# Attention in a transformer block: two score blocks at a time, with the order of every engine written out

## The chip, the cores and the metric

The kernel runs on one core of a Trainium2 chip. A core has five engines with a queue each: TensorE (PE; it multiplies matrices, and a transpose is a matmul by a permutation), VectorE (DVE), ScalarE (ACT), GpSimd (POOL) and SyncE (SP, which here only issues DMAs). Matmul results land in PSUM, 8 banks of 128 partitions by 512 floats; everything else works on SBUF. The metric is the device time of one launch, in microseconds (us), as the median of several runs.

## The reference, cut to what matters

A trunk of two layers, each a half-step SwiGLU FFN, a mixer, and another half-step FFN, on 256 tokens of width 1024. The mixer of the first layer is an SSM (Mamba-2); that of the second, which the change concerns, is attention with a window of 128 over a key and value set shared by 8 query heads (16 query heads, 2 key/value groups, head size 64):

```
q = rmsnorm((u @ w_q).reshape(b, t, KV_HEADS, GROUP, HEAD_DIM), q_norm)
...
s = einsum('bqkrd,bskd->bkrqs', qk, kk) * scale + bias
s = where(valid, s, -inf)
m = maximum(max(s), sink)
p = exp(s - m)
denom = sum(p) + exp(sink - m)
o = einsum('bkrqs,bskd->bqkrd', p / denom, vk)
...
return o @ w_o
```

The tokens fall in two tiles of 128 (t = 0, 1). Queries of tile 0 see 128 keys, those of tile 1 see 256.

## The kernel before

All activations are kept transposed, features on partitions. A weight is fetched in units of 1 MB on the SP queue, through three raw buffers, and then split by `Unit.part`: ScalarE rounds it to a high part `wh` (L171), VectorE subtracts to get the low part `wl` (L172). A product of two float32 matrices is three matmuls, high by high, high by low and low by high (`mm3`, `wmm3`). These splits run during the stage for `w_q` (16 parts of 512 columns), for `w_o` (16 parts, as soon as a part of `w_q` has been used for the last time and its buffer is free) and, after it, for the FFN.

The pages' line numbers are those of helpers: L106 is a matmul or transpose issued through `in_turn` while the order is strict, L108 one that isn't; L997 and L993 are VectorE's and ScalarE's instructions that go through `dve` and `act`.

`attention` (L946) works in these steps, for each of four query pieces (row tile t, head group g):

- `q_mm` (L953): one of eight steps k of the query product, three matmuls with 512 columns into a PSUM tile `pq`.
- `q_norm` (L961): ScalarE squares (`qn`, L963), VectorE sums by head (`ss`, L965) and adds epsilon (`me`, L220), GpSimd takes the power -1/2 (`rq`, L222), VectorE scales (`qn`, L968).
- `q_turn` (L973): four transposes into `ptq`, and ScalarE's copy to `qT` (L979).

The heads of a piece are taken in blocks (L982): a block holds 4 heads (t = 0, 128 keys) or 2 heads (t = 1, 256 keys), all of them in one half of the partitions: the two head halves i = b % 2 lie on partitions 0 to 63 and 64 to 127 of `qT` and `kT`. There are 12 blocks. For a block:

- `scores` (L999): one matmul for each head, 64 rows of the array deep, into `ps` (two PSUM buffers); then VectorE copies the sinks into the last column of `sp`, adds the bias and takes the maximum (`tensor_tensor_reduce` into `sp` and `mx`), and negates it (`nmx`).
- `expo` (L1026): ScalarE, one exponential for each head with its sum into `den`.
- `divide` (L1032): VectorE, a reciprocal `rd` and one multiplication for each head.
- `weights_T` (L1040): four transposes into `ptp` (pool `ps_tr`, two banks), ScalarE's copy to `pT`.
- `values` (L1052): matmuls of 64 columns into one half of the partitions of `po` (a bank of `ps_tr` too). After the last block of a (t, g), ScalarE rounds `po` into `uTh` and VectorE subtracts into `uTl`.

A float32 matmul of these steps shows as two matmul records in the trace, with a weight load each.

The order is written by hand at the end of `attention` (L1106 to L1131). While `strict[0]` is set, each TensorE instruction is tied behind the one before it in program order. `act` and `dve` tie ScalarE's and VectorE's instructions of the block steps in two chains in the same way; the norms and copies of the queries and the splits are in no chain, and the scheduler, which lays out each engine's queue when the program is built, puts them where it sees room. `first` gives the block steps a high priority. `F(n)` issues n pieces of filling work: 16 steps of the second head group's queries (with `q_norm` after the 8th and the 16th), then 32 pieces `o_one` of the output projection's first half (L1071), three matmuls each, which read head group 0 of `uTh` and `uTl` for both row tiles. Block n goes through scores at step n, exponentials at n+1, division at n+2, transposes at n+4, values at n+5. `fills` has no filling work for steps 6 to 10. `later(42, cur.stats)` puts the mean of squares, on which the norms rest, behind 42 matmuls.

## Time and profile before

| | us |
|---|---|
| median of 3 runs | 1043.94 (1042.96 to 1044.14) |
| the profiled execution | 1042.34 |
| its span, first to last instruction | 1040.6 |
| TensorE busy | 1028.8 (99%) |
| VectorE busy | 735.1 (71%) |
| ScalarE busy | 602.9 (58%) |
| attention, first query matmul to the second half of the output projection | 767.30 to 838.60 |

A row of the timeline gives the start in us from the first instruction, the length, the engine, the line, the operation, output<-inputs by the program's names, shapes, how many were merged (x), and in brackets the idle time before it with what ended it. PE is a matmul, PEld a weight load. A matmul's shape begins with the rows and columns of the array that it uses (64*128: half of the rows; 128*64: half of the columns). Matmuls overlap, so a matmul's own length is more than the distance to the next one's start. A row of the windows gives each engine's busy us in a stretch and its instructions (x), then TensorE's granted clock, the share of the DMA engines and GB/s. A row of the groups ends with busy us, mean ns of one, and the idle us before them with their releasers. The chain that ended last follows the end back from instruction to instruction, to whatever released each.

### The profile page before, as it was taken

What the parts mean: (1) busy time and instruction counts of PE and PEld (TensorE: products, weight loads), DVE (VectorE), ACT (ScalarE), POOL (GpSimd) and SP (SyncE); (2) the same over time, 40 slices, a digit from 0 to 9 for tenths busy, and PEclk for the clock granted to TensorE, in tenths of its full rate; (3) what the DMA queues carried; (4) which work ended last, traced back from release to release, by engine and by line L of the source; (5) the groups of instructions that cost most, each with busy time, mean ns of one, the idle gap of its engine ahead of it and who ended that gap; (6) DMA issues with size and microseconds to landing.
All of it is one profiled execution on the core that took longest, in us unless ns stands there. A gap on an engine that the chain in (4) does not pass through costs nothing.

```text
span 1040.6 us, 18036 instructions
## 1 busy us (share of the span) xinstructions
PE 1028.8 (99%) x7160; PEld 944.6 (91%) x7160; DVE 735.1 (71%) x1252; ACT 602.9 (58%) x1040; POOL 57.4 (6%) x78
## 2 busy tenths in 40 slices
PE   8899999999999999999999999999999999999998
PEld 8899999999999999999999999999996699888887
DVE  6866656789999988656556975665677678565653
ACT  6564545668976756455545754455567565455551
POOL 1100000003220010000000000100002000000000
PEclk9999999999999999999999999999999999999999
DMA  8676565658564365746465555594641436464641
GB/s 284 172 243 202 165 200 185 180 170 255 166 180 163 124 204 163 234 158 215 163 203 188 177 171 195 174 299 162 217 162 41 123 116 210 162 210 161 221 136 41
DMA packets 139589, 187.19 MB, mean 180 GB/s; under 512 B 5100, under 2 KB 122000, under 8 KB 139504
## 3 DMA queue, kind: packets, MB, share of 16 engines
q1 hardware_dynamic: 137168, 179.32, 52.8%
q0 software_dynamic: 2288, 6.69, 2.4%
q8 instruction: 56, 0.92, 0.4%
q14 instruction: 29, 0.24, 0.1%
q10 hardware_dynamic: 48, 0.02, 0.0%
HBM read 184.90 MB, written 1.11 MB: 179 GB/s over the span
## 4 chain that ended last, share of the span: by engine, by line
PE 91%; DVE 3%; DMA 3%; ACT 1%; SPq 1%; issue 0%; POOL 0%; DVEq 0%; ACTq 0%
PE pm L108 45%; PE acc L108 23%; PE pp L108 9%; PE pa L108 5%; DMA raw<-in_ffn_w_dram 2%; PE pq L106 2%; PE pa L106 1%; PE py L108 1%; DVE wl L172 1%; PE pz L108 1%; PE ps L106 1%; PE po L106 1%; DVE sp L997 1%; SPq L158 1%; PE pkv L108 1%; DMA raw<-in_ssm_w_in_dram 1%
## 5 line engine op out<-in xcount | busy, mean ns | idle before, releaser
L172 DVE TENSOR_TENSOR wl<-raw,wh 128x1024 fp32r<-128x1024 f32 (+1 forms) x372 | 412.2, 1130 | 87.3 <-ACT wh L171 86.9
L171 ACT CAST wh<-raw 128x1024 fp32r<-128x1024 f32 (+1 forms) x372 | 347.5, 970 | 110.5 <-PE acc L108 43.6
L108 PE MATMUL pm<-uT,wh 128*128 128x512 f32 (+1 forms) x1216 | 403.9, 381 | 1.7 <-DVE tp L330 1.6
L108 PE MATMUL pm<-uT,wl 128*128 128x256 f32 x1152 | 321.5, 280 | 0.0
L108 PEld LDWEIGHTS pm<-uT,wh 128*128 128x128 f32 x1216 | 223.6, 188 | 45.3 <-DVE tp L330 2.4
L108 PEld LDWEIGHTS pm<-uT,wl 128*128 128x128 f32 x1152 | 216.6, 188 | 1.0
L108 PE MATMUL acc<-ghl,wh 128*128 128x256 f32 x1056 | 190.6, 281 | 0.6 <-ACT ghl L347 0.6
L339 ACT COPY lo<-pm 128x256 f32<-128x256 f32 x136 | 50.3, 370 | 198.0 <-PE pm L108 198.0
L108 PEld LDWEIGHTS acc<-ghl,wh 128*128 128x128 f32 x1056 | 162.2, 188 | 2.9 <-ACT ghl L347 0.9
L340 DVE TENSOR_TENSOR tp<-pm,lo 128x256 f32<-128x256 f32 x136 | 57.5, 423 | 129.5 <-ACT lo L339 129.4
L108 PE MATMUL acc<-ghl,wl 128*128 128x256 f32 x528 | 148.5, 282 | 0.0
L108 PE MATMUL pp<-uT,wh 128*128 128x256 f32 x576 | 104.8, 283 | 0.1
L108 PEld LDWEIGHTS acc<-ghl,wl 128*128 128x128 f32 x528 | 99.4, 188 | 0.0
L108 PEld LDWEIGHTS pp<-uT,wh 128*128 128x128 f32 x576 | 88.8, 189 | 0.7 <-DVE uT L304 0.3
L108 PE MATMUL pp<-uT,wl 128*128 128x256 f32 x288 | 80.7, 281 | 0.0
L108 PE MATMUL pm<-vh,wh 128*128 128x256 f32 x256 | 73.3, 287 | 1.3 <-ACT wh L171 1.3
L108 PE MATMUL pm<-vh,wl 128*128 128x256 f32 x256 | 72.4, 284 | 0.5 <-DVE wl L172 0.5
L108 PE MATMUL pm<-vl,wh 128*128 128x256 f32 x256 | 72.3, 283 | 0.0
L108 PE MATMUL acc<-wh,ghl 128*128 128x512 f32 x176 | 58.3, 395 | 0.0
L108 PEld LDWEIGHTS pp<-uT,wl 128*128 128x128 f32 x288 | 54.3, 188 | 0.0
L347 ACT CAST ghl<-g 128x256 fp32r<-128x256 f32 x88 | 35.5, 403 | 31.7 <-DVE g L344 31.4
L108 PEld LDWEIGHTS pm<-vh,wh 128*128 128x128 f32 x256 | 48.9, 191 | 1.4 <-ACT wh L171 1.4
(236 smaller groups left out, 1253.5 us busy)
## 6 DMA issues: line engine op xcount, KB each, us to landing
raw<-in_ffn_w_dram SPq DMA_DIRECT2D x168, 512.0 KB, 4.9
raw<-in_ffn_w_dram SPq DMA_DIRECT2D x44, 1024.0 KB, 5.4
raw<-in_ssm_w_in_dram SPq DMA_DIRECT2D x16, 1024.0 KB, 5.5
raw<-in_ssm_w_out_dram SPq DMA_DIRECT2D x8, 1024.0 KB, 5.3
raw<-in_ssm_w_in_dram SPq DMA_DIRECT2D x8, 512.0 KB, 5.1
pr<-pdram POOLq DMA_DIRECT2D x8, 512.0 KB, 4.6
raw<-in_w_q_dram SPq DMA_DIRECT2D x4, 1024.0 KB, 5.0
raw<-in_w_o_dram SPq DMA_DIRECT2D x4, 1024.0 KB, 5.1
```

Source lines behind the costliest of these rows:

```text
L106: r = op(*args, **kw)
L108: r = op(*args, **kw)
L158: nc.sync.dma_start(view(raw, shape, lo, n0)[:, k0:k0 + src.shape[1]], src)
L171: return (nc.scalar.copy(wh, rs).ins, nc.vector.tensor_sub(wl, rs, wh.bitcast(F32)).ins)
L172: nc.vector.tensor_sub(wl, rs, wh.bitcast(F32)).ins)
L339: nc.scalar.copy(lo, pw[:, 256:512])
L340: nc.vector.tensor_add(o, pw[:, 0:256], lo)
L347: nc.scalar.copy(gh, g)
L997: chain[1] = op(*args, **kw).ins
```

## The change

Two blocks, the two head halves of the same heads, are now one pair m (six pairs). In `scores` the matmuls of the two halves alternate, head by head, into two `ps` tiles; in `values` they alternate by key tile, into the two partition halves of `po`. The sink copies move to GpSimd. `sp` and its small companions have six buffers instead of five. `po` of head group 0 lies in `ps_acc` instead of `ps_tr`. The evacuation of `po` is a step of its own (`evacuate`), written behind `expo`.

The query steps are now in the chains: the square and the copy `qT` in ScalarE's, the sums, epsilon and scaling in VectorE's. `q_norm` is cut in two, and `q_scale` is placed by hand. The first head group's query product is done row tile by row tile instead of alternating; the mean of squares comes after 26 matmuls instead of 42.

The order of steps is written out: see the end of the diff. In the loop, pair m goes through scores, then exponentials; pair m-1 is divided behind the scores of m; pair m-2 is transposed, one block on each side of the scores; pair m-3 has its values. The filling steps stand in groups of 5, 3, 4 and 4 (queries), then 10, 8, 8 and the rest (output projection).

```diff
--- before.py
+++ after.py
@@ -958,25 +958,43 @@
         def q_bank():
             return ps_acc.tile([P, 512], F32, tag="acc", name=nm("pq"))
 
+        chain = list(cur.last)
+
+        def act(op, *args, **kw):
+            with behind(chain[0]):
+                chain[0] = op(*args, **kw).ins
+
+        def dve(op, *args, **kw):
+            with behind(chain[1]):
+                chain[1] = op(*args, **kw).ins
+
         def q_norm(pq, t, n):
-            qn = ap.tile([P, 512], F32, tag="qn", name=nm("qn"), bufs=2)
-            nc.scalar.activation(qn, pq, AF.Square, scale=DH ** -0.5)
-            ss = sb.tile([P, 8], F32, tag="ss8", name=nm("ss"), bufs=2)
-            nc.vector.tensor_reduce(out=ss, in_=qn.rearrange("p (g d) -> p g d", g=8),
-                                    axis=AX.X, op=ALU.add)
-            rq = rms_rstd(ss, 8, "rq", cur.eps[:, t:t + 1])
-            nc.vector.tensor_mul(qn.rearrange("p (g d) -> p g d", g=8),
-                                 pq.rearrange("p (g d) -> p g d", g=8),
-                                 rq.unsqueeze(2).to_broadcast([P, 8, DH]))
-            qns[t, n] = qn
+            with tc.high_priority():
+                qn = ap.tile([P, 512], F32, tag="qn", name=nm("qn"), bufs=2)
+                act(nc.scalar.activation, qn, pq, AF.Square, scale=DH ** -0.5)
+                ss = sb.tile([P, 8], F32, tag="ss8", name=nm("ss"), bufs=2)
+                with behind(chain[1]):
+                    chain[1] = nc.vector.tensor_reduce(out=ss, in_=qn.rearrange("p (g d) -> p g d", g=8),
+                                                       axis=AX.X, op=ALU.add).ins
+                me = sb.tile([P, 8], F32, tag="me8", name=nm("me"), bufs=2)
+                dve(nc.vector.tensor_scalar_add, me, ss, cur.eps[:, t:t + 1])
+                rq = sb.tile([P, 8], F32, tag="rstd8", name=nm("rq"), bufs=2)
+                nc.gpsimd.tensor_tensor(out=rq, in0=me, in1=mhalf[:, :8], op=ALU.pow)
+            qns[t, n] = qn, pq, rq
+
+        def q_scale(t, n):
+            qn, pq, rq = qns[t, n]
+            with tc.high_priority():
+                dve(nc.vector.tensor_mul, qn.rearrange("p (g d) -> p g d", g=8),
+                    pq.rearrange("p (g d) -> p g d", g=8), rq.unsqueeze(2).to_broadcast([P, 8, DH]))
 
         def q_turn(t, n):
-            qn = qns[t, n]
+            qn = qns[t, n][0]
             pt = ps_acc.tile([P, 512], F32, tag="acc", name=nm("ptq"))
             for j in range(4):
                 in_turn(nc.tensor.transpose, pt[:, j * P:(j + 1) * P], qn[:, j * P:(j + 1) * P], anti)
             qT = ap.tile([P, 512], F32, tag="qT", name=nm("qT"), bufs=3)
-            nc.scalar.copy(qT, pt)
+            act(nc.scalar.copy, qT, pt)
             qTs[t, n] = qT
 
         blocks = []
@@ -986,56 +1004,48 @@
                 for b in range(8 // nh):
                     blocks.append((t, g, b, nh))
         sps, pTs, pos = {}, {}, {}
-        chain = list(cur.last)
-
-        def act(op, *args, **kw):
-            with behind(chain[0]):
-                chain[0] = op(*args, **kw).ins
-
-        def dve(op, *args, **kw):
-            with behind(chain[1]):
-                chain[1] = op(*args, **kw).ins
-
-        def scores(n):
-            t, g, b, nh = blocks[n]
+        def scores(m):
+            t, g, b, nh = blocks[2 * m]
             qT = qTs[t, g]
             L = (t + 1) * P
-            i = b % 2
             p0 = (b // 2) * nh
-            ps = ps_mm.tile([P, nh, L], F32, tag="mm", name=nm("ps"))
-            sp = ap.tile([P, nh, L + 1], F32, tag="sp", name=nm("sp"), bufs=5)
-            mx = sb.tile([P, 4], F32, tag="mx", name=nm("mx"), bufs=5)
-            nmx = sb.tile([P, 4], F32, tag="nmx", name=nm("nmx"), bufs=5)
-            den = sb.tile([P, 4], F32, tag="den", name=nm("den"), bufs=5)
-            rd = sb.tile([P, 4], F32, tag="rd", name=nm("rd"), bufs=5)
-            hs = [(p0 + x) * 2 + i for x in range(nh)]
+            pss = []
+            for i in range(2):
+                pss.append(ps_mm.tile([P, nh, L], F32, tag="mm", name=nm("ps")))
+                sps[2 * m + i] = [ap.tile([P, nh, L + 1], F32, tag="sp", name=nm("sp"), bufs=6)]
+                for w in ("mx", "nmx", "den"):
+                    sps[2 * m + i].append(sb.tile([P, 4], F32, tag=w, name=nm(w), bufs=6))
             for x in range(nh):
-                j = p0 + x
-                mm(ps[:, x, :], qT[i * DH:(i + 1) * DH, j * P:(j + 1) * P],
-                   kT[g][i * DH:(i + 1) * DH, 0:L], True, True)
-            dve(nc.vector.tensor_copy, sp[:, :, L], snk[:, g * 8 + hs[0]:g * 8 + hs[-1] + 1:2])
-            for x in range(nh):
-                hh = g * 8 + hs[x]
-                dve(nc.vector.tensor_tensor_reduce,
-                    out=sp[:, x, 0:L], in0=ps[:, x, :], in1=bias[g][:, hs[x], S - L:S],
-                    scale=1.0, scalar=snk[:, hh:hh + 1], op0=ALU.add, op1=ALU.max,
-                    accum_out=mx[:, x:x + 1])
-            dve(nc.vector.tensor_scalar_mul, nmx[:, 0:nh], mx[:, 0:nh], -1.0)
-            sps[n] = sp, nmx, rd, den
-
-        def expo(n):
-            sp, nmx, rd, den = sps[n]
-            for x in range(blocks[n][3]):
-                act(nc.scalar.activation, sp[:, x, :], sp[:, x, :], AF.Exp,
-                    bias=nmx[:, x:x + 1], accum_out=den[:, x:x + 1])
-
-        def divide(n):
-            t, g, b, nh = blocks[n]
-            L = (t + 1) * P
-            sp, nmx, rd, den = sps[n]
-            dve(nc.vector.reciprocal, rd[:, 0:nh], den[:, 0:nh])
-            for x in range(nh):
-                dve(nc.vector.tensor_scalar_mul, sp[:, x, 0:L], sp[:, x, 0:L], rd[:, x:x + 1])
+                for i in range(2):
+                    mm(pss[i][:, x, :], qT[i * DH:(i + 1) * DH, (p0 + x) * P:(p0 + x + 1) * P],
+                       kT[g][i * DH:(i + 1) * DH, 0:L], True, True)
+            for i in range(2):
+                sp, mx, nmx, den = sps[2 * m + i]
+                h0 = g * 8 + p0 * 2 + i
+                nc.gpsimd.tensor_copy(sp[:, :, L], snk[:, h0:h0 + 2 * nh - 1:2])
+                for x in range(nh):
+                    dve(nc.vector.tensor_tensor_reduce,
+                        out=sp[:, x, 0:L], in0=pss[i][:, x, :], in1=bias[g][:, (p0 + x) * 2 + i, S - L:S],
+                        scale=1.0, scalar=snk[:, h0 + 2 * x:h0 + 2 * x + 1], op0=ALU.add, op1=ALU.max,
+                        accum_out=mx[:, x:x + 1])
+                dve(nc.vector.tensor_scalar_mul, nmx[:, 0:nh], mx[:, 0:nh], -1.0)
+
+        def expo(m):
+            for n in (2 * m, 2 * m + 1):
+                sp, mx, nmx, den = sps[n]
+                for x in range(blocks[n][3]):
+                    act(nc.scalar.activation, sp[:, x, :], sp[:, x, :], AF.Exp,
+                        bias=nmx[:, x:x + 1], accum_out=den[:, x:x + 1])
+
+        def divide(m):
+            for n in (2 * m, 2 * m + 1):
+                t, g, b, nh = blocks[n]
+                L = (t + 1) * P
+                sp, mx, nmx, den = sps[n]
+                rd = sb.tile([P, 4], F32, tag="rd", name=nm("rd"), bufs=4)
+                dve(nc.vector.reciprocal, rd[:, 0:nh], den[:, 0:nh])
+                for x in range(nh):
+                    dve(nc.vector.tensor_scalar_mul, sp[:, x, 0:L], sp[:, x, 0:L], rd[:, x:x + 1])
 
         def weights_T(n):
             t, g, b, nh = blocks[n]
@@ -1049,19 +1059,23 @@
             pTs[n] = ap.tile([P, nk, nh * P], F32, tag="pT", name=nm("pT"), bufs=4)
             act(nc.scalar.copy, pTs[n], pt)
 
-        def values(n):
-            t, g, b, nh = blocks[n]
+        def values(m):
+            t, g, b, nh = blocks[2 * m]
             nk = t + 1
-            i = b % 2
             p0 = (b // 2) * nh
             if b == 0:
-                pos[t, g] = ps_tr.tile([P, 512], F32, tag="tr", name=nm("po"))
+                pool, tag = (ps_acc, "acc") if g == 0 else (ps_tr, "tr")
+                pos[t, g] = pool.tile([P, 512], F32, tag=tag, name=nm("po"))
             po = pos[t, g]
             for kk in range(nk):
-                mm(po[i * DH:(i + 1) * DH, p0 * P:(p0 + nh) * P],
-                   vtok[kk][:, g * DH:(g + 1) * DH], pTs[n][:, kk, :], kk == 0, kk == nk - 1)
-            if b == 8 // nh - 1:
-                ov = po.rearrange("p (k q) -> p k q", k=4)
+                for i in range(2):
+                    mm(po[i * DH:(i + 1) * DH, p0 * P:(p0 + nh) * P],
+                       vtok[kk][:, g * DH:(g + 1) * DH], pTs[2 * m + i][:, kk, :], kk == 0, kk == nk - 1)
+
+        def evacuate(m):
+            t, g, b, nh = blocks[2 * m]
+            if (b // 2) * nh + nh == 4:
+                ov = pos[t, g].rearrange("p (k q) -> p k q", k=4)
                 oh = uTh[:, 4 * g:4 * g + 4, t * P:(t + 1) * P]
                 act(nc.scalar.copy, oh, ov)
                 dve(nc.vector.tensor_sub, uTl[:, 4 * g:4 * g + 4, t * P:(t + 1) * P], ov, oh.bitcast(F32))
@@ -1103,31 +1117,57 @@
                     fn(*args)
             return f
 
-        Q, Sc, E, D, W, V = [first(fn) for fn in (q_turn, scores, expo, divide, weights_T, values)]
+        Q, Sc, E, D, W, V, X = [first(fn) for fn in (q_turn, scores, expo, divide, weights_T, values, evacuate)]
         with behind(*cur.last):
             nc.scalar.activation(warm, mhalf[:, 0:1], AF.Exp)
-        later(42, cur.stats)
+        later(26, cur.stats)
         strict[0] = True
         pqs = [q_bank() for t in range(NT)]
         for k in range(KT):
-            for t in range(NT):
-                q_mm(pqs[t], t, 0, k)
-        for t in range(NT):
-            q_norm(pqs[t], t, 0)
+            q_mm(pqs[0], 0, 0, k)
+        q_mm(pqs[1], 1, 0, 0)
+        q_norm(pqs[0], 0, 0)
+        q_scale(0, 0)
+        for k in range(1, KT):
+            q_mm(pqs[1], 1, 0, k)
+        Q(0, 0)
+        q_norm(pqs[1], 1, 0)
+        Sc(0)
+        q_scale(1, 0)
         F(5)
-        Q(0, 0)
-        F(1)
-        fills = (2, 2, 2, 2, 1, 1, 0, 0, 0, 0, 0, 5, 5, 5, 5, 4, 4)
-        qs = {0: (1, 0), 3: (0, 1), 7: (1, 1)}
-        lw, lv, ld = 4, 5, 2
-        last = len(blocks)
-        for n in range(last + lv):
-            for fn, m in ((W, n - lw), (V, n - lv), (Sc, n), (E, n - 1), (D, n - ld)):
-                if 0 <= m < last:
-                    fn(m)
-            F(fills[n])
-            if n in qs:
-                Q(*qs[n])
+        Q(1, 0)
+        E(0)
+        Sc(1)
+        F(3)
+        D(0)
+        q_scale(0, 1)
+        E(1)
+        F(4)
+        W(0)
+        Sc(2)
+        W(1)
+        Q(0, 1)
+        D(1)
+        F(4)
+        q_scale(1, 1)
+        E(2)
+        fills = {5: 10, 6: 8, 7: 8}
+        for m in range(3, 9):
+            if m < 8:
+                W(2 * (m - 2))
+            if m < 6:
+                Sc(m)
+            if m < 8:
+                W(2 * (m - 2) + 1)
+            V(m - 3)
+            if m == 3:
+                Q(1, 1)
+            if m < 7:
+                D(m - 1)
+            if m < 6:
+                E(m)
+            X(m - 3)
+            F(fills.get(m, 0))
         F(32)
         strict[0] = False
         nxt.open()
```

## The prediction

> **What bounds the kernel now.** I read the page first: how busy TensorE is, and who carries the chain that ended last.
>
> ```profile
> PE 1028.8 (99%) x7160; PEld 944.6 (91%) x7160; DVE 735.1 (71%) x1252; ACT 602.9 (58%) x1040; POOL 57.4 (6%) x78
> ...
> PE 91%; DVE 3%; DMA 3%; ACT 1%; SPq 1%; issue 0%; POOL 0%; DVEq 0%; ACTq 0%
> ```
>
> TensorE carries 91% of the end. The change touches only the attention stage, so I cut that stage into four stretches in the table of windows: A, the queries of the first head group (767.30 to 778.80 us); B, up to the last matmul of the second group's queries; C, which has no filling work; D, in which half of the output projection fills the gaps, up to its second half at 838.60.
>
> ```profile
> core 0: us, PE busy (x) PEld busy (x) DVE busy (x) ACT busy (x) POOL busy (x), PEclk, DMA share, GB/s
> 767.30:778.80 11.50, 11.50 (x56) 9.57 (x55) 7.61 (x19) 6.80 (x14) 0.71 (x1) 1.00 0.41 155
> 778.80:801.54 22.74, 22.07 (x103) 15.53 (x102) 17.41 (x70) 14.72 (x45) 4.88 (x3) 1.00 0.14 48
> 801.54:819.28 17.74, 17.02 (x81) 9.98 (x79) 17.06 (x75) 15.43 (x48) 1.64 (x1) 1.00 0.40 120
> 819.28:838.60 19.32, 19.32 (x133) 15.53 (x133) 5.18 (x21) 6.23 (x15) 0.00 (x0) 1.00 0.18 55
> ```
>
> In A, B and D TensorE is the bound. In C it looks busy (17.02 of 17.74), but VectorE is too (17.06), and the chain in order of time says which of the two counts:
>
> ```profile
> 767.56 9.56 PE pq L106 x42
> ...
> 799.76 1.06 PE ps L106 x4
> ...
> 801.80 0.61 ACT qn L963
> ...
> 804.84 0.27 DVE sp L997
> ...
> 805.66 0.60 DVE qn L968
> 806.26 0.08 DVE nmx L997
> 806.34 0.07 DVE rd L997
> 806.40 0.59 DVE wl L172
> ...
> 814.04 0.40 DVE sp L997
> ```
>
> Behind the last query matmuls (the first two lines are TensorE's) the chain leaves TensorE, runs over ScalarE's square at 801.80, and stays on VectorE for most of C: the score reductions (0.27 us for 128 keys, 0.40 for 256), divisions, norms, and also the splits of the next weights (wl, L172, 0.59 each). A split slips in wherever an attention step needs the result of the step just before it, as here between the reciprocal and its division. So C is already VectorE's, and time taken from TensorE there is worth nothing by itself.
>
> **The change part by part.** *Halves in turn.* Prices of one block's scores, transposes and values, each from its start to the next start in the timeline (the last line is values again, of a block with 256 keys):
>
> ```profile
> 802.07 1.07 PE L106 MATMUL po<-pT,v 128*64 128x512 f32 x2
> 803.07 1.16 PE L106 MATMUL ps<-kT,qT 64*128 64x128 f32 x8
> 804.16 0.66 PE L106 MATMUL ptp<-anti,sp 128*128 128x128 f32 x4
> 804.74 1.08 PE L106 MATMUL po<-pT,v 128*64 128x256 f32 x4
> ```
>
> Scores 1.09 (for 256 keys 1.06, in the chain above), values 1.00, transposes 0.58: 12 blocks cost 25 us in scores and values. Every block uses one half of the array. Two column halves side by side do occur in this trace, in the SSM stage (lines 772 to 776 write py in two halves of 64 columns):
>
> ```profile
> 264.70 1.98 PEld L108 LDWEIGHTS py<-em,xdt 128*64 128x64 f32 x24
> 264.70 2.22 PE L108 MATMUL py<-em,xdt 128*64 128x256 f32 x24
> ```
>
> These 24 are half 256 and half 128 columns wide. At the prices above (1.08 us for four of 256, 1.16 for eight of 128) one after the other they would take 3 x 1.08 + 1.5 x 1.16 = 5.0 us; they take 2.22. So a values pair costs about one block: 6 x 1.0 = 6.0 us saved. For row halves (scores) no row exists. The bounds are 0 and 6 x 1.09 = 6.5 us; I take 6.4, as the py rows are the nearest. On TensorE that is up to 12.4 us.
>
> [...]
>
> *A: the first row tile's eight steps before the second's.* A step of three matmuls takes 3 x 9.56/42 = 0.68 us (the 42 in the chain above). Step k=7 of row tile 0 was the 15th, about 776.9; now it is the 8th, at 772.1. It needs the last splits of w_q, which VectorE makes behind the norm's own work:
>
> ```profile
> 773.23 1.29 DVE L172 TENSOR_TENSOR wl<-raw,wh 128x512 fp32r<-128x512 f32 x2
> ```
>
> In the order of the parts these two, the last, are k=7's for the first and for the second head group. Step k=7 waits for the first of them, done half way, at 773.9; the matmul that reads it would have started at 772.3. TensorE waits about 1.6 us, a wait that the old order hid, and queued behind it is everything on TensorE. The mean of squares (now after nine steps) is ready by then. In return the first norm chain runs under the other tile's seven steps (4.8 us). A becomes 13.1 us, +1.6.
>
> *B.* Query turns, and the scores straight behind them:
>
> ```profile
> 783.04 0.63 PE L106 MATMUL ptq<-anti,qn 128*128 128x128 f32 x4 [0.67 <-DVE qn L968]
> ...
> 784.35 1.16 PE L106 MATMUL ps<-kT,qT 64*128 64x128 f32 x8
> ```
>
> Turn to scores is 1.31 us, of which the turn's slots are 0.55; a filling step lay in between. Now pairs 0 and 1 follow their turns bare: 2 x 0.75 us idle. TensorE's list for B: 16 steps 10.9, turns 3 x 0.55, scores 3 x 1.09, transposes 2 x 0.55, idle 1.5 for the turns and about 0.6 at the first division and at restarts of filling: 19.0, against 22.74. That is -3.7, of which 1.0 is the first values group moved into C.
>
> *C.* This is the part that decides. Prices for it, and for the sink copies, from the groups of the stage (busy us, then mean ns):
>
> ```profile
> L993 ACT ACTIVATE sp<-sp,nmx 128x257 f32<-128x257 f32 x16 | 8.0, 507 | 1.1 <-DVE nmx L997 1.1
> ...
> L997 DVE TENSOR_SCALAR sp<-sp,rd 128x256 f32<-128x256 f32 x16 | 4.9, 352 | 0.1
> ...
> L997 DVE COPY sp<-snk 128x2 f32<-128x2 f32 x8 | 1.3, 165 | 0.0
> ...
> L222 POOL TENSOR_TENSOR rs<-me,mhalf 128x2 f32<-128x2 f32 x1 | 0.7, 712 | 99.6 <-DVE eps L286 99.6
> ```
>
> In VectorE's written order the scaling of the last query tile stands ahead of pair 3's reductions, these ahead of the division of pair 2, and TensorE's order waits for each. C' starts at 767.3 + 13.1 + 19.0 = 799.4. The last norm took 801.80 to 806.26, 4.5 us, in the chain; division 1 and one split stand ahead of its reduction, about 1.0: scaled at 804.9. Pair 3: 8 x 0.27, two negations 0.15, and two splits in their holes 1.2: 808.4. Division of pair 2, reciprocal, a split, two halves (4.9/16 = 0.31 each): transposes start at 809.7, and TensorE, with 3.7 us of work since 799.4, has idled some 6 us. Next round: transposes 0.55, scores 1.09, reductions 4 x 0.40 + 0.15, two splits 1.2, reciprocal and split 0.7, first division and handover 0.4: 5.7 us, 815.4. Last round: 1.64 to the end of the scores, 1.0 to the first negation, exponentials of four heads 2.1 (4 x 0.507), and only then (the evacuation is written behind them) ScalarE's copy (about 0.6, as its square of the same 512 columns) and VectorE's subtraction (about 0.6, as a split), with handovers 0.4: 821.7. The output projection reads both row tiles of that result, so its first matmul waits for this. C' is 22.3 us, +4.6.
>
> Seven splits stand in this walk (1 + 2 + 1 + 2 + 1). Each takes 0.59 where an idle of some 0.1 would be without it. Bounds: with none of them C' is about 7 x 0.5 = 3.5 shorter; with two more, 1 longer. I take one in each such hole, as the chain above shows it.
>
> *D.* TensorE has no idle there: 32 filling steps, four blocks' transposes and five blocks' values make up the 19.32. Three values pairs (3.0) now do for the five blocks (5.0); two waits for a bank may add 0.2: -1.8.
>
> *The sink copies* leave VectorE (12 of them at 0.17 us or less: up to 2.0) and go to GpSimd, where no such copy is in the trace; nearest is the 0.71 us row above, so 0 to 0.7 each. They wait only for a free sp buffer, of which there are six now, so they lie far ahead of the exponentials: nothing. Without that cover an exponential waits 0.7. The values of the first head group in another pool leave two banks to the transposes; I count nothing for it. Nothing is moved past a DMA queue.
>
> Sum: +1.6 - 3.7 + 4.6 - 1.8 = +0.7 us on the profiled execution, which took 1042.34 us (span 1040.6 and 1.7 around): 1043.0. The median of the runs, 1043.94, lies 1.6 above that execution; so 1044.6.
>
> **The rivals.** *One: the splits get out of the way* (faster). If the scheduler puts them into B or D, where VectorE has room (5.18 of 19.32 busy in D), C' loses 3.5, and if k=7's part also comes in time, 1.6 more: 1044.6 - 5.1 = 1039.5. For it: only four splits are needed when filling starts. Against it: in C now they sit in these holes. Chance 0.27. *Two: TensorE's whole saving arrives*, 12.4 - 1.6 - 1.5 = 9.3: 1043.94 - 9.3 = 1034.6. For it, 91% of the chain is TensorE; against it, C's chain. 0.05. *Three: row halves don't run at once* (slower). Place: each scores pair; price 6.4 us on TensorE, about half in front of C's waits, which then shrink: +3.3, 1047.9. It decides from 1.7 us for a pair on. For it: no row shows row halves. 0.18. *Four: C's rounds are longer than walked* (handovers, further splits), +3: 1047.6, 0.10. *Five: column halves take turns*: the three values pairs in D cost 3.0 more, those in C stand beside VectorE's work: 1047.6; against it the py rows, 0.02. That the written order is not kept can hardly be, since each instruction is tied to the one before it; it is in four. The forecast itself, within 0.2% (2.1 us, about what a measurement of this kernel can tell from none): 0.38.
>
> **How the numbers follow.** Faster 0.27 + 0.05 = 0.32, same 0.38, slower 0.18 + 0.10 + 0.02 = 0.30. The range takes in one, three and four with a part of their spread and leaves out two: 1038.8 to 1048.5. The forecast's own range is 1042 to 1046.
>
> **What would show it.** Right: an idle of 1.6 us before a wl in the first query tile; scores pairs of about 1.1 us with twice the matmuls; bare waits for qT; VectorE solid behind the last query norm, TensorE idle 10 us or more in all up to the output projection, whose first matmul waits for uT. Wrong: scores pairs of 2 us (three), few wl rows among C's divisions (one), or TensorE without long waits in C (two).

## The result, and the profile after

The changed kernel takes 1051.08 us (median of four runs, 1047.87 to 1052.29), the kernel before 1043.45 (1042.77 to 1044.14): ratio 1.0064, 95% interval 1.0053 to 1.0076. Measured again with six runs it is 1049.93 against 1044.19, 1.0056 (1.0040 to 1.0071). It is slower by 0.6%. The forecast was 1044.6, with a range that ended at 1048.5.

In 11 of the 15 profiles TensorE's clock stands at half for 3.4 or 6.8 us some 42 to 45 us after the start (in after for 6.83 us from 42.11), far ahead of the change. The profile of before is one without it, that of after one with it. For the other runs only the mean clock is on record: of 70 further runs of before, 55 had 0.998 or less (median 1044.1 us) and 15 had 0.999 or more (1042.6), so it is probably there in most of them, at a cost of some 2 us. I therefore compare the stage by its own length, from the first query matmul to the first matmul of the output projection's second half. That is 767.40 to 838.43 before, 71.0 us, and 769.87 to 848.09 after, 78.2. Behind it both take 202 us. So the stage lost 7.2 us, and the forecast for it was +0.7.

The page of the kernel after, in the lines shown of before, with the granted clock by slices:

```profile
PE 1025.4 (98%) x7160; PEld 945.6 (90%) x7160; DVE 734.9 (70%) x1240; ACT 602.5 (57%) x1040; POOL 60.4 (6%) x90
...
PEclk9899999999999999999999999999999799999999
...
PE 90%; DVE 4%; DMA 2%; ACT 2%; SPq 1%; issue 0%; POOL 0%; DVEq 0%; ACTq 0%; POOLq 0%
```

TensorE is busy 3.4 us less than before, and the kernel is longer. The 7 in the clock's row is the slice from 814 to 840 us, inside the attention stage. The table of windows, cut at A, B, C and D as they lie now:

```profile
769.87:782.90 13.03, 11.70 (x54) 9.34 (x53) 8.88 (x20) 6.80 (x13) 2.36 (x2) 1.00 0.36 138
782.90:801.70 18.80, 17.44 (x101) 13.25 (x99) 13.26 (x59) 12.70 (x39) 3.61 (x4) 1.00 0.01 1
801.70:827.20 25.50, 14.08 (x80) 8.64 (x80) 21.58 (x82) 18.72 (x59) 2.92 (x5) 0.80 0.52 165
827.20:848.09 20.89, 20.11 (x133) 17.33 (x134) 3.46 (x9) 4.30 (x9) 0.00 (x0) 0.84 0.00 1
```

A (13.0) and B (18.8) came as forecast (13.1 and 19.0). C is 25.5 us where 22.3 was forecast, D 20.9 where 17.5 was forecast. In both, and only there, the clock (the third number from the end) is below 1.00. TensorE's own rows, with the idle before them in brackets:

```profile
776.39 0.50 PE L106 MATMUL pq<-wl,vh 128*128 128x512 f32 x1 [1.33 <-DVE wl L172]
784.19 1.16 PE L106 MATMUL ps<-kT,qT 64*128 64x128 f32 x16 [0.68 <-ACT qT L965]
796.76 1.13 PE L106 MATMUL ps<-kT,qT 64*128 64x256 f32 x8
802.59 0.63 PE L106 MATMUL ptp<-anti,sp 128*128 128x128 f32 x4 [0.90 <-DVE sp L969]
808.19 0.63 PE L106 MATMUL ptq<-anti,qn 128*128 128x128 f32 x4 [2.29 <-DVE qn L969]
812.63 1.09 PE L106 MATMUL ptp<-anti,sp 128*128 128x128 f32 x4 [3.81 <-DVE sp L969]
813.65 2.08 PE L106 MATMUL ps<-kT,qT 64*128 64x256 f32 x8
820.21 1.01 PE L106 MATMUL ptp<-anti,sp 128*128 128x128 f32 x4 [2.33 <-DVE sp L969]
827.26 1.30 PE L106 MATMUL pa<-uT,wh 128*128 128x256 f32 x2 [2.16 <-ACT uT L965]
```

A scores pair of 16 records takes 1.16 us, as one block of 8 did: the halves run at once. The waits are those that the prediction walked. But a scores pair of 256 keys, which takes 1.13 us at 796.76, takes 2.08 at 813.65, and four transposes 1.09 instead of 0.63. Stretches of 3.41 us, at the edges where the clock changes, show why:

```profile
806.70:810.11 3.41, 0.63 (x4) 0.42 (x4) 2.76 (x14) 1.97 (x5) 0.76 (x2) 1.00 0.00 0
810.11:813.52 3.41, 0.89 (x4) 0.72 (x4) 3.41 (x15) 3.41 (x18) 0.00 (x0) 0.50 0.71 221
813.52:816.94 3.42, 3.42 (x15) 2.14 (x16) 3.29 (x7) 2.11 (x6) 0.23 (x2) 0.50 0.37 102
816.94:820.35 3.41, 1.08 (x10) 0.51 (x8) 3.34 (x16) 2.11 (x8) 0.27 (x1) 1.00 0.98 316
820.35:823.76 3.41, 3.41 (x15) 2.30 (x15) 1.76 (x10) 1.09 (x4) 0.00 (x0) 0.50 0.87 288
823.76:827.18 3.42, 1.34 (x11) 0.56 (x9) 2.90 (x14) 3.00 (x10) 0.00 (x0) 1.00 0.01 3
827.18:830.59 3.41, 3.19 (x13) 2.90 (x14) 2.07 (x7) 0.02 (x1) 0.00 (x0) 0.50 0.00 0
```

Each stretch here in which TensorE (first busy time) works little (0.63, 0.89, 1.08, 1.34 us) is followed by one at half clock (0.50), so TensorE pays for an idle twice: once while it waits, once in the next 3.41 us. In all, 17.1 us of the stage run at half clock, in three stretches of 6.83, 3.41 and 6.83 us. My prediction had no term for it. On VectorE, meanwhile:

```profile
813.33 0.61 DVE L969 TENSOR_SCALAR sp<-sp,rd 128x256 f32<-128x256 f32 x2
814.07 0.69 DVE L969 TENSOR_TENSOR uT<-po,uT 128x512 fp32r<-128x512 f32 x1
814.68 2.49 DVE L172 TENSOR_TENSOR wl<-raw,wh 128x512 fp32r<-128x512 f32 x4
817.08 0.48 DVE L969 CUSTOM_DVE_ANT_0 sp<-ps,bias,snk 128x256 f32<-128x256 f32 x1
```

Four splits in a row stand ahead of the reductions of the fifth scores pair, for which TensorE, ScalarE and the next transposes wait.

### The profile page after: what moved, and what is told of

The parts are those of the page before. It is cut to its first block, busy times and chain, and to the rows that moved or that the text cites. A ratio compares the mean times of both kernels' runs of the same rounds, so it can differ in the third digit from the quotient of the medians.

```text
span 1050.6 us, 18053 instructions
## 1 busy us (share of the span) xinstructions
PE 1025.4 (98%) x7160; PEld 945.6 (90%) x7160; DVE 734.9 (70%) x1240; ACT 602.5 (57%) x1040; POOL 60.4 (6%) x90
## 4 chain that ended last, share of the span: by engine, by line
PE 90%; DVE 4%; DMA 2%; ACT 2%; SPq 1%; issue 0%; POOL 0%; DVEq 0%; ACTq 0%; POOLq 0%
PE pm L108 44%; PE acc L108 22%; PE pp L108 10%; PE pa L108 5%; DMA raw<-in_ffn_w_dram 2%; DVE wl L172 2%; PE pa L106 1%; PE pq L106 1%; PE py L108 1%; PE pz L108 1%; ACT wh L171 1%; SPq L158 1%; PE pkv L108 1%; ACT sp L965 0%; DVE sp L969 0%
## 5 line engine op out<-in xcount | busy, mean ns | idle before, releaser
L108 PE MATMUL acc<-ghl,wh 128*128 128x256 f32 x1056 | 192.8, 284 | 0.3 <-ACT ghl L347 0.3
L339 ACT COPY lo<-pm 128x256 f32<-128x256 f32 x136 | 50.3, 370 | 201.0 <-PE pm L108 201.0
L108 PE MATMUL pm<-vh,wl 128*128 128x256 f32 x256 | 72.4, 283 | 0.3 <-DVE wl L172 0.3
L108 PEld LDWEIGHTS pp<-uT,wl 128*128 128x128 f32 x288 | 54.4, 189 | 0.0
```

The lines of the kernel that those rows point to most:

```text
L108: r = op(*args, **kw)
L339: nc.scalar.copy(lo, pw[:, 256:512])
```

## The experiments

Theory one: the idle of C turns the clock down, and that is the 6 us. Theory two: VectorE's walk of C is longer than forecast, and the clock is a bystander. All ratios are to the kernel before on the same chip, "half" is the time at half clock in the stage of the profiled run (for the two hole kernels, in and behind the hole).

| kernel | median us | ratio (95% interval) | stage us | half us |
|---|---|---|---|---|
| before | 1043.7 to 1044.2 | | 71.0 | 0 |
| after, again | 1049.93 | 1.0056 (1.0040, 1.0071) | 78.1 | 17.1 |
| fed | 1047.16 | 1.0025 (1.0015, 1.0035) | 74.2 | 0 |
| fed_lean | 1046.63 | 1.0024 (1.0015, 1.0033) | 73.9 | 0 |
| fed_front | 1049.23 | 1.0046 (1.0031, 1.0062) | 78.0 | 10.2 |
| seq | 1048.99 | 1.0051 (1.0034, 1.0069) | 78.4 | 17.1 |
| late7 | 1048.16 | 1.0039 (1.0027, 1.0052) | 75.5 | 13.7 |
| split | 1044.80 | 1.0010 (1.0001, 1.0019) | 72.4 | 10.2 |
| fed_split | 1043.62 | 1.0000 (0.9991, 1.0009) | 71.6 | 0 |
| early | 1042.49 | 0.9983 (0.9973, 0.9993) | 70.0 | 6.8 |
| ahead | 1036.69 | 0.9926 (0.9912, 0.9940) | 63.1 | 0 |
| ahead_split | 1033.60 | 0.9904 (0.9889, 0.9919) | 61.1 | 0 |
| hole_short | 1052.09 | 1.0083 (1.0068, 1.0097) | | 6.8 |
| hole_long | 1058.28 | 1.0142 (1.0128, 1.0156) | | 13.7 |

**again**: no edit. 

> The changed kernel as it is, beside the others on one chip. Theory one (the clock): the idle of TensorE in C (0.90, 2.29 and 3.81 us within 10 us, 4.91 us busy of 11.90) makes the throttle halve its clock for some 17 us, and the stage, which took 78.2 us against 71.3 before, owes about 6 us to that. The half clock should then stand in C again, at 810 to 834 us give or take 3, while the half clock at 42 to 49 us, far ahead of the change, may or may not be there. 1051 us, 1048 to 1053. Theory two (the walk): the stage is longer because VectorE's chain of rounds is, and the clock is a bystander: the same time, and the stage at 78 us with or without records of a half clock in C. If the clock stays at 1.0 in C and the stage still takes 78 us, theory one falls.

The half clock begins at 808.4, 818.6 and 825.5 us, 1.7 us earlier than in the first profile; the stage starts 1.5 us earlier. It recurs in the same places.

**fed**: matmuls that nobody needs, in the idle of C.

```diff
+        def feed(bank, n):
+            for _ in range(n):
+                mm(bank, anti, anti, True, True)
...
+            if (t, n) == (1, 1):
+                feed(pt[:, 0:P], 12)
...
+            feed(pt[:, 0, 0:P], {2: 4, 4: 22, 6: 13}.get(n, 0))
...
+                    feed(accs[0][:, 0:P], 12)
```

> The changed kernel with 63 matmuls of 128 columns more, of the exchange matrix with itself, into banks that the next real matmul overwrites: 4 ahead of the transposes of block 2, 12 ahead of the last query turn, 22 ahead of the transposes of block 4, 13 ahead of those of block 6 and 12 ahead of the first filling step of the output projection, each a little less than the idle that stood there (0.90, 2.29, 3.81, 2.33 and 2.16 us, at about 0.15 us for one). They change no dependency of the other engines. Theory one: the clock stays at 1.0 in C, the steps that ran at half clock take their old time (eight scores matmuls of 256 columns 1.1 us instead of 2.08), and the stage falls from 78.2 to about 72 us: 1045 us, 1044 to 1046.5. Theory two: VectorE's rounds stay as they are, so the fillers change nothing or stand in the way: 1051 us or up to 2 more.

The same times in both kernels, after first, then fed (whose stage begins 3.3 us earlier):

```profile
802.00:814.00 12.00, 5.31 (x38) 3.49 (x40) 10.41 (x40) 10.56 (x36) 2.58 (x4) 0.84 0.51 165
802.00:814.00 12.00, 12.00 (x101) 10.21 (x98) 10.47 (x36) 9.59 (x30) 4.13 (x4) 1.00 0.51 168
```

The clock stays at 1.00 and the stage loses 3.9 us: more work on TensorE makes the kernel faster. That speaks for theory one, but 3 us over before were left, where one was expected. Part of it is the fillers' own: one took 0.24 us, not 0.15, and block 4's transposes began 1.2 us late.

**fed_lean**: 4, 8, 16, 12 and 8 of them. 

> The kernel with fillers, with fewer of them. One took 0.24 us in the run before (12 in 2.94 us), not 0.15, so that the transposes of block 4 stood ready at about 809.5 and began at 810.7, 1.2 us late. Now 4, 8, 16, 12 and 8 instead of 4, 12, 22, 13 and 12. Theory one (the clock): it still stays at 1.0, and the stage falls from 74.2 to about 72.8 us: 1045.8 us, 1044.8 to 1046.8, with a stage 1.5 to 2 us longer than before, which is what is left for the walk of the rounds. Theory two (the walk alone): the stage is as long as VectorE's chain, so fewer fillers change nothing (1047) or the clock falls back and it is 1049.

The clock stays at 1.00, block 4's transposes begin in time, and the stage is 73.9, not 72.8: of the 1.4 us that these gained, 0.4 are left at block 6's. VectorE's rows between them:

```profile
813.76 1.29 DVE L172 TENSOR_TENSOR wl<-raw,wh 128x512 fp32r<-128x512 f32 x2
814.96 0.69 DVE L969 TENSOR_TENSOR uT<-po,uT 128x512 fp32r<-128x512 f32 x1
815.56 0.68 DVE L172 TENSOR_TENSOR wl<-raw,wh 128x512 fp32r<-128x512 f32 x1
816.16 0.48 DVE L969 CUSTOM_DVE_ANT_0 sp<-ps,bias,snk 128x256 f32<-128x256 f32 x1
```

The fifth scores pair began at 813.08; its first reduction, at 816.16, stood behind three splits. In the list of VectorE eleven splits stand between the last query norm's reduction and the output projection, here as in after; one lies under the norm's power on GpSimd, where it costs nothing, and ten are in the walk. The sum puts six of its seven there, so four more stand in the way than it has. So theory one alone falls: part of the miss is the walk. D takes 18.2 us at full clock against 20.9 in after; these 2.7 us are the clock's.

```profile
825.50:843.69 18.19, 17.26 (x133) 14.58 (x133) 3.44 (x9) 4.31 (x8) 0.00 (x0) 1.00 0.00 1
```

**fed_front**: fillers 4, 8, 16 and no others. 

> Fillers in the first half of C alone: 4 ahead of block 2's transposes, 8 ahead of the last query turn, 16 ahead of block 4's transposes; the idle ahead of block 6's transposes (2.3 us) and of the filling (2.2 us) is left open. It asks which idle turns the clock down. If the stretch from 801 to 810 us does it (3.81 us without a matmul, under half busy), the clock stays at 1.0 to the end of the stage and the time is that of the lean fillers, 1045.8 us. If the two later gaps, 4.5 of 11 us, are enough, the clock falls some 10 us later, at about 820 us, the filling runs at half clock for a while, and it is 1047.5 to 1049 us.

The second case. The two later gaps are enough (3.4 of the 10.2 us at half clock are another stretch, in A):

```profile
816.88:820.29 3.41, 1.12 (x8) 0.89 (x10) 3.34 (x17) 2.39 (x9) 0.00 (x0) 1.00 0.54 179
820.29:823.71 3.42, 3.42 (x18) 1.98 (x16) 2.24 (x12) 1.27 (x3) 0.00 (x0) 0.50 0.83 282
```

**seq**: the halves one after the other.

```diff
-            for x in range(nh):
-                for i in range(2):
+            for i in range(2):
+                for x in range(nh):
                     mm(pss[i]
...
-            for kk in range(nk):
-                for i in range(2):
+            for i in range(2):
+                for kk in range(nk):
                     mm(po[i
```

> The changed kernel with the halves one after the other again: all scores of one block of a pair, then all of the other, and the same for the values. All else is as in the change. TensorE then takes about 1.1 us more for each scores pair and 1.0 more for each values pair: 3.3 in A and B, 3.0 in D, and in C some of its idle is filled. Theory one: with more of C busy the clock falls less or not at all, so about 6 us come back of the 6.3 that are lost: 1050 us, 1048.5 to 1052, with a granted clock nearer to 1.0 in C. Theory two: 1056 to 1058 us, since the walk of C is as long and B and D are longer.

Both theories started from a false premise: TensorE takes hardly more. A pair of 128 keys takes 1.71 us instead of 1.16,

```profile
782.88 1.71 PE L106 MATMUL ps<-kT,qT 64*128 64x128 f32 x16 [0.68 <-ACT qT L965]
```

and scores pairs of 256 keys and values pairs the same as in turn (32 records of 256 columns of po take 4.4 us in both). So for the halves to run at once it was enough here that the two blocks stand next to each other in TensorE's order; taking turns saves a further 0.55 us (1.71 against 1.16), in each of the two pairs of 128 keys. This run tells the theories apart in nothing else.

**late7**: the last step of the first query tile behind two of the second's.

```diff
-        for k in range(KT):
+        for k in range(KT - 1):
             q_mm(pqs[0], 0, 0, k)
         q_mm(pqs[1], 1, 0, 0)
+        q_mm(pqs[1], 1, 0, 1)
+        q_mm(pqs[0], 0, 0, KT - 1)
```

> The changed kernel with one edit in A: step k=7 of the first query tile, which waits 1.33 us for the last part of w_q, stands behind the second step of the other tile. Both theories: the wait goes, and everything behind it moves up by 1.3 us: 1048.6 us, 1048 to 1049.3, with the half clock in C as before. If it gives nothing, the first norm was what the stage waited for, and the term of 1.6 us in the prediction was no cost of its own.

The first turn comes 1.36 us earlier from the stage's start (11.68 against 13.04), and 1.2 us of it are left at the projection. The stage gains 2.6, twice as much as the wait, since one stretch at half clock is gone from D. The stretch at half clock that reaches into the filling has 3.26 us of work in it here and the clock comes back (from 828.1 on a filling step takes 0.35 us, before it 0.64); in after it has 3.19, and the clock stays at 0.50 for another 3.41 us. So here it counted where the stretches of 3.41 us begin against the work, and an edit worth 1.2 us gave 2.6.

**split**: ten of w_o's sixteen splits tied behind the evacuation that ends C, the last step on VectorE ahead of the filling (in the trace they stand behind uT at 821.30).

```diff
-                uo.append(row_unit(a["w_o"][0], i * 256))
+                uo.append(row_unit(a["w_o"][0], i * 256, hold=i > 0))
+            for i, c in ((1, 0), (1, 1024), (1, 512), (1, 1536)) + tuple(
+                    (i, c) for i in (2, 3) for c in range(0, 2048, 512)):
+                u = uo[i]
+                wh, wl = u.get(c, 512)
+                nc.scalar.copy(wh, u.raw[:, c:c + 512])
+                with behind(*(chain[1:] if (i, c % 1024) != (1, 0) else ())):
+                    nc.vector.tensor_sub(wl, u.raw[:, c:c + 512], wh.bitcast(F32))
```

> The changed kernel with one edit: ten of the sixteen splits of the output projection's weights (w_o) that make wl on VectorE are tied behind the first evacuation, so that they leave VectorE's list in C. In the kernel with lean fillers eleven splits of 0.6 us stood in C behind the last division of pair 1, four of them ahead of the fifth scores pair's reductions, where the prediction had counted seven, two there. If they are what the walk is longer by, C loses some 2.5 us. By theory one the idle of TensorE shrinks with them, and part of the half clock may go as well: 1045 to 1048 us against 1050. By theory two in its plain form (VectorE's chain is the whole loss) C loses the same and more: 6 us, 1044. If the splits filled holes alone: no change, 1050.

Some 5 us come back, near theory two's figure. Behind the last norm's reduction one split is left in C, inside the norm; the fifth pair's reductions follow the first evacuation at once:

```profile
811.86 0.69 DVE L969 TENSOR_TENSOR uT<-po,uT 128x512 fp32r<-128x512 f32 x1 [1.49 <-ACT uT L965]
812.64 0.48 DVE L969 CUSTOM_DVE_ANT_0 sp<-ps,bias,snk 128x256 f32<-128x256 f32 x1
```

But 10.2 us at half clock stay, so the clock costs much less here than with the splits in.

**fed_split**: both edits. 

> The same edit in the kernel with lean fillers, where the clock stayed at 1.0 and the stage took 73.9 us against 71.0 before. If the further splits are what was left over, the stage falls to 71.5 to 72.5 us (the prediction's own walk gave 71.9), the time from 1046.6 to about 1044.9: then clock and splits account for the whole miss. If the fillers themselves were in the way, or D is longer for another reason, it stays above 73. The splits may come late for the filling or push back the next loads; the stretch behind the stage, 202.2 us, would then be longer.

The time is that of before: what the change lost is gone with clock and splits. The stage, 71.6 us, is also what the prediction's sum gives, 71.0 + 0.7 = 71.7, but that is chance. The sum has seven splits in its walk, 3.5 us, while ten are out of it here; and the fillers now stand in the way. The chain that ended last runs over TensorE, fillers included, from 806.26 to 819.99 us, and block 6's transposes follow the start of their division by 1.52 us, in split by 0.48: about 1 us is the fillers' own.

The four kernels give both prices. With the splits in C, the clock's half speed costs 78.1 - 73.9 = 4.2 us; without them 72.4 - 71.6 = 0.8, or about 1.8 if the fillers' 1 us is taken off. With the clock free to fall, the splits cost 78.1 - 72.4 = 5.7 us; at full clock 73.9 - 71.6 = 2.3, or about 3.3. So the two overlap by some 2.4 to 3.4 us: the splits lengthen the idle, and the idle slows the clock. Together they are worth 6.5 us or a little more.

**early**: another written order behind the third scores pair. The first of its new lines, with W to X as in the change:

```diff
+        E(2)
+        F(4)
+        D(2)
+        q_scale(1, 1)
+        W(2)
+        Sc(3)
+        W(3)
+        V(0)
+        E(3)
+        V(1)
+        W(4)
+        W(5)
+        Q(1, 1)
+        V(2)
+        X(0)
+        X(2)
+        Sc(4)
+        D(3)
+        E(4)
+        F(6)
...
```

> The changed kernel in another written order behind the third scores pair: the division of pair 2 stands ahead of the last query scaling on VectorE, the values of pairs 0, 1 and 2 follow as soon as their transposes are made, so that the first head group is evacuated before the fourth scores pair of the second tile, and the 32 filling steps (0.353 us each) are spread in groups of 6, 6, 7, 7 and the rest over the last two scores pairs and the last divisions. The long waits of C (3.81 ahead of block 4's transposes, 2.33 ahead of block 6's, 2.16 ahead of the filling) are then partly covered by filling. Theory one: with no stretch of 10 us in which TensorE is busy less than half, the clock stays at 1.0, and TensorE's saving of some 12 us less about 5 of idle arrives: 1036 to 1039 us. Theory two: VectorE's chain sets the end also in this order, the divisions and reductions are the same number, and filling only moves the wait: 1044 to 1048 us.

Between the two. The order was wrong in one place: E(3) stands ahead of the copies of blocks 4 and 5 on ScalarE. TensorE waits 5.01 us for them and the next 6.8 run at half clock:

```profile
813.10 2.45 PE L106 MATMUL po<-pT,v 128*64 128x256 f32 x8 [5.01 <-ACT pT L965]
...
809.04:812.45 3.41, 0.00 (x0) 0.00 (x0) 3.41 (x14) 3.18 (x16) 0.00 (x0) 1.00 0.49 166
812.45:815.87 3.42, 2.77 (x10) 1.49 (x12) 2.67 (x5) 2.33 (x7) 0.00 (x0) 0.50 0.77 249
```

**ahead**: that mended, late7 taken in, and filling between turns and scores. Against early, without late7's lines and the last filling groups:

```diff
+        Sc(3)
         W(2)
-        Sc(3)
         W(3)
         V(0)
-        E(3)
         V(1)
...
         X(2)
         Sc(4)
+        E(3)
         D(3)
...
+        F(1)
         Q(0, 0)
         q_norm(pqs[1], 1, 0)
+        F(1)
         Sc(0)
...
```

> The reordered kernel once more. In it the exponentials of pair 3 stood ahead of the copies of blocks 4 and 5 on ScalarE, and TensorE idled 5.01 us ahead of their values; half clock began there at 812.45. Now the exponentials stand behind the copies and the first evacuation, the fourth scores pair of the tile ahead of the transposes of block 2 and the fifth behind the values, step k=7 of A is held back as in the run beside, and a filling step stands between each of the first two query turns and its scores. Theory one: no idle over 2 us is left, the clock stays at 1.0, and the stage is about 63 to 65 us against 71: 1036 to 1039 us. Theory two: VectorE's 46 us of work in the stage are no bound for 63, but if its chain of divisions and reductions sets the end whatever TensorE's order, it stays at 1041 to 1043.

As theory one had it: 0.74% faster than before, the stage 8 us shorter. The stretch that was C is 12 us, and the filling starts at 807.65:

```profile
766.89:795.60 28.71, 27.38 (x148) 21.55 (x147) 20.57 (x72) 17.80 (x49) 5.96 (x6) 1.00 0.17 62
795.60:807.65 12.05, 11.01 (x72) 6.57 (x70) 12.05 (x47) 11.96 (x34) 3.21 (x5) 1.00 0.53 174
807.65:829.94 22.29, 19.99 (x150) 16.26 (x150) 13.82 (x52) 12.67 (x38) 0.00 (x0) 1.00 0.30 96
```

The pairs' saving on TensorE was in the changed kernel too (1.13 to 1.16 us a scores pair). Here the first head group's values and evacuation stand ahead of the second group's last scores, so that the filling covers VectorE's rounds. What late7's edit and the regrouped filling give of the 8 us was not measured one by one.

**ahead_split**: with the edit of split. 

> The same edit in the kernel that is ordered once more (1036.7 us, stage 63.05). There TensorE waits for VectorE only 0.4 us here and there ahead of the filling, so the splits in the holes cost little: 1035.5 to 1037 us. If they delay the filling or the next loads, up to 2 us slower.

1033.60 us, 1.0% faster than before and more than expected: the stage loses another 2.0 us, half of it ahead of the filling (11.05 us where ahead has 12.05).

**hole_short, hole_long**: the kernel before, with a wait put in behind the filling, eight or seventeen copies long; the second half of the output projection is kept in written order behind it.

```diff
         F(32)
+        scr = ap.tile([P, 512], F32, tag="qn", name=nm("scr"), bufs=2)
+        for _ in range(8):
+            act(nc.scalar.copy, scr, bias[1][:, 0:2, :].rearrange("p i s -> p (i s)"))
+        ph = ps_mm.tile([P, P], F32, tag="mm", name=nm("ph"))
+        mm(ph, scr[:, 0:P], anti, True, True)
...
+            strict[0] = True
             for d in (2 * b, 2 * b + 1):
                 for k in range(4, KT):
                     o_one(1, d, k)
+            strict[0] = False
```

> The kernel before the change, with a hole made in TensorE's work at the end of the stage: eight more copies of 512 columns on ScalarE (0.48 us each, from the rows of two in 1.07) behind the last evacuation, and one matmul that waits for the last of them, between the filling of the output projection and its second half. TensorE then idles about 1.8 us. Theory one: such a hole leaves every stretch of 3.4 us with 1.6 us of work or more, the clock stays at 1.0, and the kernel is slower by the hole alone: 1.8 us, 1045.5. Theory two says the same of this run.

> The same with seventeen copies: TensorE idles about 6 us, and at least one stretch of 3.4 us is all but empty. Theory one: the clock is at 0.5 in the next one or two stretches, with plain matmuls ahead and behind and no walk of VectorE's in the way, and costs half of these: 1.7 to 3.4 us on top of the 6, so 1051.4 to 1053.2. Theory two (the clock is a bystander): the hole alone, 1049.7.

The holes came out as 6.18 and 12.03 us, since casts of the next weights stand among the copies, so the short one isn't the test it was to be. Both show the price:

```profile
846.30 0.80 PE L106 MATMUL ph<-anti,scr 128*128 128x128 f32 x2 [6.18 <-ACT scr L993]
...
838.49:841.90 3.41, 1.63 (x14) 1.43 (x13) 1.59 (x2) 3.32 (x5) 0.00 (x0) 1.00 0.00 0
841.90:845.32 3.42, 0.00 (x0) 0.00 (x0) 2.94 (x3) 3.39 (x6) 0.00 (x0) 1.00 0.36 104
845.32:848.73 3.41, 2.43 (x11) 2.43 (x12) 0.37 (x1) 0.90 (x2) 0.00 (x0) 0.50 1.05 355
```

With no walk of VectorE's near, a stretch without work (0.00 us) is followed by one at 0.50; in hole_long, one with 0.29 us (838.91 to 842.33) is, too. The time rose by 8.0 us for 6.18 of idle and by 14.2 for 12.03: 1.8 and 2.2 us more than the idle, of which the waiting matmul itself is 0.45. Theory two had nothing more than the idle.

## Why the prediction was wrong, step by step

*A* was right: a wait of 1.33 us for the split (1.6 forecast), 13.0 us in all (13.1); late7 takes it away. *B* was right: bare waits of 0.68 and 0.67 us (0.75 each), 18.8 us (19.0). *The halves*: right, a scores pair 1.13 to 1.16 us, eight values matmuls of 256 columns 1.08; rivals three and five fall. *The sink copies* cost nothing: 0.18 to 0.46 us each on GpSimd, and no engine waits for them. The signs that the prediction set for being right are in the trace, in the main; none of them looks at the clock.

*C* failed ("C' is 22.3 us, +4.6"). Counted from the stage's start, the last query turn was forecast at 37.6 us and came at 38.3, block 4's transposes at 42.4 and 42.8: right so far. Block 6's came at 50.3 instead of 48.1, and the projection at 57.4 instead of 54.4. At full clock (fed_lean) it came at 55.7, so 1.7 of the 3.0 are the clock and 1.3 are not. These 1.3 arise between block 4's transposes and block 6's: 7.2 us at full clock, 5.7 forecast. The scores there were done at 814.1, and their first reduction began at 816.16, because three splits and the first evacuation (0.6 us) stand between it and the division ahead on VectorE. The sum lets the reductions follow the scores at once: it has no split at that place, and the evacuation, which VectorE's written order puts there, is not in it. In split, with those splits out, the same round took 5.8 us, although TensorE was at half clock. This is a part of rival four.

*D* failed mostly by the clock: 20.9 us against 17.5; 6.8 us of it run at half clock, where a filling step takes 0.64 us instead of 0.35. At full clock (fed_lean) D was 18.2, with 0.9 us of waits (0.34 for uT, twice 0.29 for pT) where 0.2 were forecast.

So the step that failed is the price of idle in C. The prediction saw the idle ("has idled some 6 us"; the five long waits up to the projection add up to 11.5, and 10 or more were forecast) and took it to cost only itself. Its sum has no term for the clock, which cost 78.2 - 73.9 = 4.3 of the 6.5 us that the stage is over the forecast; the unforeseen splits and evacuation ahead of one round's reductions are most of the rest. Rival one was the right lever with too low a price: it had 3.5 us for seven splits, and taking ten out gave 5.7, more than 2 us of it because less idle also saves clock.

What stays open: why the further splits stand just there in VectorE's list (the written order ties the attention steps to one another and leaves the splits to the scheduler), and how long the changed kernel would take at full clock without splits and without fillers, which no run has.

## What to carry to other kernels

In these runs a wait on TensorE cost itself and, where it left a stretch of 3.41 us with little work (0.00 to 1.48 us at full clock), more at half clock: 1.8 and 2.2 us beyond the idle of the two holes, 0.45 of it the waiting matmul. A reordering that packs TensorE's work tighter and pools its idle can lose by that what it gained, as this one did. Before trusting such a change, look at the granted clock by windows, and spread the work that nobody waits for over the holes. When the order of an engine is written out by hand, what is left to the scheduler there (here the splits) lands between the written steps and belongs in the order as well.

## What the runs showed of the hardware

- Cutting the traces of before and after, between 5 and 1030 us, into stretches of 3.41 us at the clock's own edges, and counting TensorE's busy time at half clock half: in after, seven stretches have 0.45 to 1.60 us of such work, and each was followed by one at half clock (0.50); the others have 1.71 us or more, and none was. In before the lowest is 1.84, and the clock stays at 1.00. Of the other runs' stretches shown, 1.63 us in hole_short (838.49 to 841.90) was followed by 1.00, and 2.07 in fed_front's A (772.51 to 775.92) by 0.50; why is open.
- At half clock, 3.41 us busy of 3.41 in after and 3.26 in late7 were followed by full clock, 3.19 and 3.14 in after by half clock again.
- Two blocks on different row or column halves of the array ran at once also when one is written right after the other: in seq, scores of 256 keys (32 records in 6.5 us, in after 6.4) and values pairs (1.08 to 1.09 us) lost next to nothing, and pairs of 128 keys took 1.71 us instead of 1.16.
- Matmuls of 128 columns of float32 into one bank, one behind the other, took some 0.24 us each in fed (twelve in 2.94 us).
